# Average pooling over a row: loads and stores issued from GpSimd in place of SyncE

## The chip, the cores and the metric

The kernel runs on one core of a Trainium2 chip. The metric is the device time of one execution in microseconds (us), as the median of several runs. A profiled execution gives the trace; its "span" is the time from the first to the last recorded instruction. In the profile the engines are called PE (TensorE), DVE (VectorE), ACT (ScalarE), POOL (GpSimd) and SP (SyncE). A name with a q at the end, such as SPq or POOLq, is the sequencer of that engine, which handles instructions that are not computation: waits, barriers and the issue of DMA transfers.

## The reference

The input x is 32 x 256 x 4096 in float32, 134.2 MB. Each row of 4096 is cut into 256 windows of 16 neighbours, and the output holds the mean of every window, 32 x 256 x 256, 8.4 MB.

```python
def reference(x, output_size):                     # output_size = 256
    ...
    for i in range(output_size):
        start = int(i * length / output_size)
        end = int((i + 1) * length / output_size)
        result[:, :, i] = np.mean(x[:, :, start:end], axis=-1)
```

## The kernel before

The 32 x 256 = 8192 rows are worked off in 16 tiles of 512 rows. A tile has 128 partitions with 4 rows (65,536 bytes) each, so one load moves 8.39 MB. In SBUF a tile is seen as 128 partitions x 1024 windows ("cells") x 16 elements. The pool `inpool` has two buffers of that size, and the loads go to them in turn: load t + 2 needs the buffer of load t.

The loop `for t in range(ntiles)` does the following for each tile:

- line 70 issues the load into `xin`, on SP;
- line 73, on POOL, folds the second half of the windows (cells 512 to 1023): the upper 8 elements of each window are added onto the lower 8;
- line 78, on DVE, sums the 16 elements of each window in the first half;
- line 81, on DVE, sums the 8 remaining elements of each window in the second half, and so waits for line 73;
- line 84, on ACT, multiplies the tile's 1024 sums by 1/16.

The first fifteen tiles write their results into one large buffer, `res_many`, which a single store of 7,680 KB takes out. This store stands in the last turn of the loop, in the text between the load of the last tile and the computation on it. The last tile writes into `res_last`, and two stores, of 120 and of 8 partitions, take that out after the loop. All three stores go through the helper `store` (line 58). It issues the DMA, excludes it from the semaphores that the tile framework manages (`no_tile_sem_insts`) and lets it raise a semaphore of its own, `stored`, by 16.

The tile framework records the instructions while the kernel's text runs. When the context is compiled (`tc.compile()`), it fixes the order of each engine's queue and puts in the waits. Each engine then works its queue off in that order. In the kernel before, SP's queue holds only the issues of the loads and stores, and POOL's queue only the adds of line 73, apart from constants at the start and the closing barrier, which the profile shows under line 94. After that barrier SP waits until `stored` has reached 48, that is, until all three stores have landed, and clears it.

Of the kernel before, what the change touches and what calls it, by code (L numbers as in the profile page):

```python
# [1 line left out]

# [4 lines left out]


@with_exitstack
def kernel(  # L10
    ctx: ExitStack,
    tc: tile.TileContext,
    x: bass.AP,
    output_size: int,
    out: bass.AP,
):

    nc = tc.nc
    F32 = mybir.dt.float32
    X = mybir.AxisListType.X

    batch, channels, length = x.shape
    ob, oc, olen = out.shape
    assert ob == batch and oc == channels and olen == output_size
    assert length % output_size == 0
    window = length // output_size  # L30
    hw = window // 2
    inv_w = 1.0 / float(window)

    P = nc.NUM_PARTITIONS
    R = 4
    rows = batch * channels
    assert rows % (P * R) == 0
    ntiles = rows // (P * R)
    many = (ntiles - 1) * R
    cells = R * output_size  # L40
    m = cells // 2
    cols = R * length

    xr = x.rearrange("b c l -> (b c) l")
    orow = out.rearrange("b c o -> (b c) o")
    x_many = xr[0 : P * many, :].rearrange("(p r) l -> p (r l)", p=P, r=many)
    o_many = orow[0 : P * many, :].rearrange("(p r) o -> p (r o)", p=P, r=many)
    x_last = xr[P * many :, :].rearrange("(p r) l -> p (r l)", p=P, r=R)
    o_last = orow[P * many :, :].rearrange("(p r) o -> p (r o)", p=P, r=R)

    res_many = nc.alloc_sbuf_tensor("res_many", [P, (ntiles - 1) * cells], F32, align_bytes=256)
    res_last = nc.alloc_sbuf_tensor("res_last", [P, cells], F32, align_bytes=256)
    inpool = ctx.enter_context(tc.tile_pool(name="inpool", bufs=2))

    stored = nc.alloc_semaphore("stored")

    def store(out, in_):
        ins = nc.sync.dma_start(out=out, in_=in_)
        tc.no_tile_sem_insts.add(ins.ins.name)
        ins.then_inc(stored, 16)  # L60

    for t in range(ntiles):
        last = t == ntiles - 1
        xin = inpool.tile([P, cells, window], F32, name="xin")
        if last:
            res, base, src = res_last, 0, x_last
        else:
            res, base = res_many, t * cells
            src = x_many[:, t * cols : (t + 1) * cols]
        nc.sync.dma_start(out=xin.rearrange("p o w -> p (o w)"), in_=src)  # L70
        if last:
            store(o_many, res_many[:, :])
        nc.gpsimd.tensor_add(  # L73
            out=xin[:, m:cells, 0:hw],
            in0=xin[:, m:cells, 0:hw],
            in1=xin[:, m:cells, hw:window],
        )
        nc.vector.reduce_sum(  # L78
            out=res[:, base : base + m], in_=xin[:, 0:m, :], axis=X
        )  # L80
        nc.vector.reduce_sum(  # L81
            out=res[:, base + m : base + cells], in_=xin[:, m:cells, 0:hw], axis=X
        )
        nc.scalar.mul(  # L84
            out=res[:, base : base + cells],
            in_=res[:, base : base + cells],
            mul=inv_w,
        )
    for lo, hi in ((0, 120), (120, P)):
        store(o_last[lo:hi, :], res_last[lo:hi, :])  # L90

    ctx.pop_all().close()
    tc.close()
    tc.compile()  # L94
    nc.sync.wait_ge(stored, 48)
    nc.sync.sem_clear(stored)


# [1 line left out]
_INS = ['x', 'output_size']  # L100
_OUTS = [((32, 256, 256), 'float32')]

_NUMBERS = {'output_size': 256}


# [26 lines left out]
```

## Time and profile before

| what | value |
|---|---|
| median of 3 runs | 333.5 us (333.32 to 333.67) |
| the profiled execution | 333.37 us, its span 332.1 us |
| DVE busy | 209.7 us, 63% of the span |
| POOL busy | 139.7 us, 42% |
| ACT busy | 18.2 us, 5% |
| HBM read and written | 134.22 MB and 8.39 MB, 429 GB/s over the span |

Busy time counts computing instructions only; waits, barriers and the issue of a DMA do not count. "DMA share" is the mean busy share of the core's 16 DMA engines. In lists of waits, a line names the instruction that waited, what released it, the total time, how often, and the longest. A row for an instruction group gives the shape of output and input, the count, the busy time and the mean of one. A load's "time to landing" runs from its issue to the signal that its data has arrived. These are the groups of computing instructions in the loop:

```profile
L73 POOL TENSOR_TENSOR xin<-xin 128x4096 f32<-128x4096 f32 x16 | 139.5, 8719 | 181.7 <-DMA xin<-in_x_dram 181.7
L78 DVE TENSOR_REDUCE res_many<-xin 128x512 f32<-128x8192 f32 x15 | 130.3, 8686 | 107.4 <-DMA xin<-in_x_dram 107.4
L81 DVE TENSOR_REDUCE res_many<-xin 128x512 f32<-128x4096 f32 x15 | 66.3, 4420 | 2.5 <-POOL xin L73 2.3
L84 ACT ACTIVATE res_many<-res_many 128x1024 f32<-128x1024 f32 x15 | 15.9, 1057 | 289.8 <-DVE res_many L81 289.8
```

### The profile page before, as it was taken

What the parts mean: (1) busy time and instruction counts of PE and PEld (TensorE: products, weight loads), DVE (VectorE), ACT (ScalarE), POOL (GpSimd) and SP (SyncE); (2) the same over time, 40 slices, a digit from 0 to 9 for tenths busy, and PEclk for the clock granted to TensorE, in tenths of its full rate; (3) what the DMA queues carried; (4) which work ended last, traced back from release to release, by engine and by line L of the source; (5) the groups of instructions that cost most, each with busy time, mean ns of one, the idle gap of its engine ahead of it and who ended that gap; (6) DMA issues with size and microseconds to landing.
All of it is one profiled execution on the core that took longest, in us unless ns stands there. A gap on an engine that the chain in (4) does not pass through costs nothing.

```text
span 332.1 us, 160 instructions
## 1 busy us (share of the span) xinstructions
DVE 209.7 (63%) x32; ACT 18.2 (5%) x17; POOL 139.7 (42%) x20
## 2 busy tenths in 40 slices
DVE  0029396692939669293966939295693929569392
ACT  1000101001010100101010010101000010100001
POOL 0027091542709164270916427090643709063270
DMA  9898999989899998989899998989999898989997
GB/s 379 379 505 379 474 411 426 458 379 505 379 489 395 450 434 379 505 379 505 379 474 411 395 489 379 505 379 489 395 450 434 379 505 379 505 379 474 395 466 307
DMA packets 2599, 142.61 MB, mean 429 GB/s; under 512 B 295, under 2 KB 295, under 8 KB 423
## 3 DMA queue, kind: packets, MB, share of 16 engines
q1 hardware_dynamic: 2599, 142.61, 99.4%
HBM read 134.22 MB, written 8.39 MB: 429 GB/s over the span
## 4 chain that ended last, share of the span: by engine, by line
DMA 66%; POOL 18%; DVE 11%; POOLq 3%; issue 0%; ACT 0%; SPq 0%
DMA xin<-in_x_dram 66%; POOL xin L73 18%; DVE res_many L81 9%; POOLq L94 3%; DVE res_last L81 1%; ACT res_last L84 0%; SPq L70 0%; POOLq L73 0%
## 5 line engine op out<-in xcount | busy, mean ns | idle before, releaser
L73 POOL TENSOR_TENSOR xin<-xin 128x4096 f32<-128x4096 f32 x16 | 139.5, 8719 | 181.7 <-DMA xin<-in_x_dram 181.7
L78 DVE TENSOR_REDUCE res_many<-xin 128x512 f32<-128x8192 f32 x15 | 130.3, 8686 | 107.4 <-DMA xin<-in_x_dram 107.4
L81 DVE TENSOR_REDUCE res_many<-xin 128x512 f32<-128x4096 f32 x15 | 66.3, 4420 | 2.5 <-POOL xin L73 2.3
L84 ACT ACTIVATE res_many<-res_many 128x1024 f32<-128x1024 f32 x15 | 15.9, 1057 | 289.8 <-DVE res_many L81 289.8
L78 DVE TENSOR_REDUCE res_last<-xin 128x512 f32<-128x8192 f32 x1 | 8.7, 8686 | 6.3 <-DMA xin<-in_x_dram 6.3
L81 DVE TENSOR_REDUCE res_last<-xin 128x512 f32<-128x4096 f32 x1 | 4.4, 4420 | 0.2 <-POOL xin L73 0.2
L84 ACT ACTIVATE res_last<-res_last 128x1024 f32<-128x1024 f32 x1 | 1.1, 1057 | 18.5 <-DVE res_last L81 18.5
L84 ACT ACT_TABLE_LOAD x1 | 1.3, 1283 | 0.7 <-PEq L113 0.7
L113 POOL MEMSET const-float32-0.0<- 128x1 f32 x1 | 0.1, 99 | 0.2 <-issue 0.2
L113 POOL MEMSET const-bfloat16-1.0<- 128x1 bf16 x1 | 0.1, 103 | 0.0
L113 POOL MEMSET const-uint8-127<- 128x1 uint8 x1 | 0.1, 103 | 0.0
L113 POOL MEMSET const-float32-1.0<- 128x1 f32 x1 | 0.1, 99 | 0.0
## 6 DMA issues: line engine op xcount, KB each, us to landing
out_dram<-res_many SPq DMA_DIRECT2D x1, 7680.0 KB
out_dram<-res_last SPq DMA_DIRECT2D x1, 480.0 KB
xin<-in_x_dram SPq DMA_DIRECT2D x16, 25.3
out_dram<-res_last SPq DMA_DIRECT2D x1, 32.0 KB
```

The source lines that it names most:

```text
L73: nc.gpsimd.tensor_add(out=xin[:, m:cells, 0:hw], in0=xin[:, m:cells, 0:hw], in1=xin[:, m:cells, hw:window],)
L78: nc.vector.reduce_sum(out=res[:, base : base + m], in_=xin[:, 0:m, :], axis=X)
L81: nc.vector.reduce_sum(out=res[:, base + m : base + cells], in_=xin[:, m:cells, 0:hw], axis=X)
L84: nc.scalar.mul(out=res[:, base : base + cells], in_=res[:, base : base + cells], mul=inv_w,)
L94: tc.compile()
L113: nc = _bacc.Bacc("TRN2", target_bir_lowering=False, num_devices=1)
```

## The change

The two places that issue a DMA, the helper `store` and the load in the loop, name GpSimd in place of SyncE. What is moved, the shapes, the two buffers and the computation stay as they are. SP keeps the wait for `stored` and its clearing at the end.

```diff
     def store(out, in_):
-        ins = nc.sync.dma_start(out=out, in_=in_)
+        ins = nc.gpsimd.dma_start(out=out, in_=in_)
         tc.no_tile_sem_insts.add(ins.ins.name)
         ins.then_inc(stored, 16)
...
-        nc.sync.dma_start(out=xin.rearrange("p o w -> p (o w)"), in_=src)
+        nc.gpsimd.dma_start(out=xin.rearrange("p o w -> p (o w)"), in_=src)
```

## The prediction

> **What bounds the kernel now.** I read the table of queues first, then stretches of the timeline with their DMA share, then the waits of SP's own queue beside the chain of waits, and last the instructions at both ends. The queue and the stretches:
>
> ```profile
> q1 hardware_dynamic: 2599, 142.61, 99.4%
> 22.70:42.00 19.30, 13.11 (x2) 1.06 (x1) 8.72 (x1) 1.00 1.00 435
> 42.00:312.90 270.90, 183.52 (x29) 14.80 (x14) 122.07 (x14) 1.00 1.00 433
> 327.30:332.10 4.80, 0.00 (x0) 0.00 (x0) 0.00 (x0) 1.00 0.74 314
> ```
>
> The columns of the last three rows are the length of the stretch, the busy time of DVE, ACT and POOL with counts, PE's clock, the DMA share and GB/s. In the loop the 16 DMA engines are always busy, at 433 to 435 GB/s. The add of load 1 starts at 42.05 us and that of load 15 at 312.97, so one load takes 270.92 / 14 = 19.35 us. DVE has 13.1 us of work per load and POOL 8.7; neither sets that pace. What SP waits for, one period of the chain in order of time, and the loads themselves:
>
> ```profile
> SPq L70 <- DVE res_many L81: 185.8, 14, 13.3
> ...
> 80.72 0.02 issue
> 80.74 0.02 POOLq L73
> 80.76 0.09 issue
> 80.85 8.73 POOL xin L73
> 89.58 0.02 issue
> 89.60 4.43 DVE res_many L81
> 94.03 0.02 issue
> 94.05 25.30 DMA xin<-in_x_dram
> ...
> L70 SPq DMA_DIRECT2D xin<-in_x_dram x16: 327/328/413, 0.7 to 287.3; - x16
> DMA to landing us min/median/max: 22.0/25.3/40.8
> ```
>
> The load of this period has landed at 80.72, and its buffer is released 94.05 - 80.72 = 13.3 us later. The next load is then in flight for another 19.35 - 13.3 = 6.0 us. So each issue comes 6.0 us before the engines would run dry, and 25.3 us to landing is 6.0 of queueing plus 19.35 of transfer. The shortest time to landing, 22.0 us with nothing ahead, leaves 22.0 - 19.35 = 2.7 us for issue, first bytes and the semaphore. These 2.7 us are covered by the 6.0 in the loop; 3.3 us of cover remain.
>
> **The change part by part.** The sum is made against the profiled execution: span 332.1, time 333.37, so 1.3 us lie around the span; 333.37 is 0.13 below the median of 333.5.
>
> First, removed: nineteen issues on SP (sixteen loads at 0.33 to 0.41 us, one store at 0.35, two at 0.74 together). SP computes nothing and nobody waits for it but the DMA, so this gives back only what stands at the ends. The same nineteen issues are added to POOL's queue, which already holds sixteen adds.
>
> Second, the price of one issue on POOL, which no row shows. From below: POOL's shortest instruction, MEMSET, 0.10 us, so a gain of 0.3 at the first load. From above: POOL's longest, the add, 8.72 us, a loss of 8.4. The nearest row is the same operation on SP, 0.41 at the first load; since it is not the same engine I raise the fixed 2.7 us by a quarter: 0.7 us more than on SP, about 1.1 per issue. At the first load nothing covers it, because all engines idle until the first landing: +0.7.
>
> Third, the fourteen later loads. Their wait for DVE's release moves to POOL's queue. If load t+2 stands there between add t and add t+1, POOL waits at it from the end of add t (landing + 8.75) to the release (landing + 13.3), issues in about 1.1 us, and has 19.35 - 13.3 - 1.1 = 4.9 us left before add t+1 can start. Queued behind the wait is only that add, and DVE's second reduction waits for it; neither is late. The added 0.7 lies under the 3.3 us of cover: 0. With the cover gone each microsecond counts fourteen times. At the upper bound an issue is 8.4 longer, 5.1 beyond the cover, or 14 x 5.1 = 71 us.
>
> Fourth, the big store. In the timeline its data is ready at 307.67, load 15 lands at 312.86 and add 15 cannot begin earlier: 5.2 us of cover against 1.1. Cost 0.
>
> Fifth, the end. These rows are the last issues, the drains of the closing barrier and SP's last wait:
>
> ```profile
> 327.26 0.74 SPq L58 DMA_DIRECT2D out_dram<-res_last  x2
> ...
> L94 SPq EVENT_SEMAPHORE  x6: 17/28/28, 328.1 to 329.0; - x6
> L94 POOLq DRAIN  x3: 34/83/8811, 312.9 to 328.8; - x3
> L94 SPq DRAIN  x3: 7/7/7, 328.3 to 328.6; - x3
> ...
> SPq L96 <- DMA out_dram<-res_last: 3.0, 1, 3.0
> ```
>
> The big store, 7,680 KB, occupies the engines for 7.86 MB / 434 GB/s = 18.1 us from 312.86, so to about 331.0. The two small stores, issued at 327.26, only have to stand in the queue by then: 3.7 us of cover against twice 1.1, cost 0. The barrier is different. Now it runs from 328.1 to 329.0 while the stores are still moving, and SP's wait of 3.0 us comes after it. POOL's drain in this barrier is a new risk. From below: SP's drain takes 7 ns with SP's own stores in flight, so a drain need not wait for DMAs: 0. From above: POOL's drain held 8,811 ns, until POOL's last add was over; if it likewise holds until the DMAs that POOL issued are through, the whole barrier moves behind the last landing: 329.0 - 328.1 = +0.9. I take the upper value, because that row is of the same engine. What is late next is only SP's clear of the semaphore.
>
> Sum: 0.7 + 0 + 0 + 0 + 0.9 = 1.6; 333.37 + 1.6 = 335.0, and on the median 333.5 + 1.6 = 335.1.
>
> A rule speaks against the change. The adds take 8,717 to 8,722 ns in all sixteen cases, each beside a DVE reduction of 8.69 us, and DVE is idle for 6.0 us when a later load is issued. The Trainium skill (SBUF — State Buffer, section "SBUF: two separate sides") says that a DMA issued from GpSimd is starved of descriptors while VectorE holds the shared port in a 2-port mode. No row here shows such blocking; were it to hold for these reductions, the moment of issue would still miss them, and the sum would stay. The same skill (DMA: Bandwidth & Descriptors, "Latency and other measured facts") puts the first byte at about 1 us from GpSimd and 600 ns from SP; by it the first term would be 0.4 and the time 334.8, an estimate from that page.
>
> **The rivals.** The decisive unknown is the order in POOL's queue, which the build fixes and the page of before cannot show, since there the loads stand alone on SP. My forecast takes it that the framework queues an instruction when what it needs is there, so that load 1 comes before add 0 and load t+2 before add t+1.
>
> Rival one, pairs: two loads, then two adds. Load 2, free at landing 0 + 13.3, then stands behind add 1, which begins only at the next landing. For: nothing in the page forbids it. Against: add 1 has to wait 6.0 us longer than load 2. It decides as soon as a load stands behind an add that waits for a later landing. Price: the engines run dry and start again 8.73 (add) + 22.0 (alone to landing) + 0.7 after the landing, that is 31.4 in place of 19.35, +12.1 once per pair, so 7 x 12.1 = 85 us: 420; if the big store stands behind add 15 as well, 8.7 + 2.7 + 0.7 = 12 more: 432. I put it at 426.
>
> Rival two, the order of the text: load, add, load, add. It is how the loop is written. Every later load pays 12.1: 15 x 12.1 = 181, so 335 + 181 = 516.
>
> Rival three, software pace: the order is good, but an issue or the packets that it makes are dearer. The whole 8.72 at the first load gives 333.5 + 8.4 + 0.9 = 343; packets 2% slower cost 16 x 19.35 x 0.02 = 6, so 341. Against: the page shows 435 GB/s with packets of 65 KB (142.61 MB in 2,599), so little is decided per packet.
>
> Rival four, on the other side: not slower. Place: the two ends. POOL's issue costs no more than SP's 0.41 us and its drain no more than SP's 7 ns; the price is 0 and the time 333.5. It decides when both terms together stay under 0.67 us. For: SP's drain row. Against: POOL's. That the change doesn't do what it says is no case here: the two edited calls are the only issues there are.
>
> **How the numbers follow.** Chances: forecast 0.61, own range 334.0 to 336.8 (from a third of the sum to about twice the sum above 333.5); rival one 0.11, rival two 0.08, rival three 0.09, rival four 0.11. The time is the forecast's, 335.1. The range reaches down to rival four with the scatter of the runs, 333.1, and up through rival three with both its prices a little exceeded, 346; outside are rivals one and two, 0.19. A measurement of this kernel can tell about 0.2%, 0.67 us, from no change. Slower is above 334.17: 0.59 of the forecast's 0.61, and rivals one to three, 0.28; together 0.87. Same, 332.83 to 334.17: 0.02 of the forecast and 0.08 of rival four, 0.10. Faster: the rest of rival four, 0.03, where POOL's issue comes at its lower bound.
>
> **What would show it.** The order is seen at once: the second load issued within some 2 us of the first, the adds 19.35 us apart, the DMA share at 1.00 in the loop. A first landing at about 23.4 in place of 22.7 shows the first term. A barrier after the last landing, POOL's long drain ending there and SP's wait near 0 show the last. Adds alternately 31 and 19 us apart mean rival one, all 31 apart rival two, an even pace above 19.4 rival three. The forecast is wrong above all if a load stands behind an add.

## The result, and the profile after

The changed kernel takes 465.93 us as a median (465.88 to 466.14) against 333.51 before: a ratio of 1.397, 95% interval 1.395 to 1.400. The forecast was 335.1, its range 333.1 to 346.

The page of the changed kernel, engines and queue:

```profile
DVE 208.2 (45%) x32; ACT 18.2 (4%) x17; POOL 150.2 (32%) x39
q0 software_dynamic: 2624, 142.61, 72.2%
```

The same 142.61 MB now keep the DMA engines busy for 72.2% of the span, where it was 99.4%. The profile lists POOL's queue as `software_dynamic` and the one that SP used before as `hardware_dynamic`. The busy time of DVE and ACT is as before, and POOL has only gained the issues, 39 instructions in place of 20: on POOL the profile does count an issue as busy time, 10.5 of the 150.2 us, unlike on SP. So no computation has grown; time has been added in which nothing moves. One period of the loop in stretches (length, busy time of DVE, ACT, POOL with counts, PE's clock, DMA share, GB/s):

```profile
42.80:56.10 13.30, 13.30 (x3) 0.25 (x1) 8.72 (x1) 1.00 0.00 0
56.10:78.20 22.10, 4.07 (x2) 1.86 (x2) 1.10 (x2) 1.00 1.02 427
78.20:97.50 19.30, 8.67 (x2) 0.00 (x0) 8.71 (x1) 1.00 0.88 380
```

For 13.3 us after the landing at 42.80 the DMA share is 0.00. A load with nothing ahead of it then takes 22.1 us from issue to landing, and a second one lands 19.3 us later. Two loads take 54.8 us ((426.34 - 42.80) / 7, from landing 1 to landing 15) in place of 38.7. The timeline shows what the first of them waited for:

```profile
42.80 8.69 DVE L78 TENSOR_REDUCE res_many<-xin 128x512 f32<-128x8192 f32 x1 [10.60 <-DMA xin<-in_x_dram]
42.85 8.72 POOL L73 TENSOR_TENSOR xin<-xin 128x4096 f32<-128x4096 f32 x1 [10.57 <-DMA xin<-in_x_dram]
51.40 8.74 DVE L81 TENSOR_REDUCE res_many<-xin 128x512 f32<-128x4096 f32 x2
55.85 1.06 ACT L84 ACTIVATE res_many<-res_many 128x1024 f32<-128x1024 f32 x1 [53.82 <-DVE res_many L81]
56.11 0.58 POOL L70 DMA_DIRECT2D xin<-in_x_dram  x1 [4.54 <-DVE res_many L81]
...
60.44 0.53 POOL L70 DMA_DIRECT2D xin<-in_x_dram  x1 [3.76 <-DVE res_many L81]
...
78.17 8.69 DVE L78 TENSOR_REDUCE res_many<-xin 128x512 f32<-128x8192 f32 x1 [18.03 <-DMA xin<-in_x_dram]
```

Tile 0 landed at 23.51 and was added by 32.3, yet its second sum (line 81) does not run until 51.4, together with that of tile 1 ("x2"). DVE's queue holds the first sum of tile 1 ahead of it, and that one waits for landing 1. Only at 55.8 is the buffer of tile 0 free. On POOL, load 2 stands behind add 1, which also waits for landing 1. This is POOL's queue as listed from the built programs (+ added, - removed; ISA is the instruction that the trace calls MODIFY_POOL_CONFIG):

```
+L70 DMACopy xin<-in_x_dram 128x16384 x2
 L73 ISA
-L73 TensorTensor xin<-xin 128x512x8 x16
+L73 TensorTensor xin<-xin 128x512x8 x2
+L70 DMACopy xin<-in_x_dram 128x16384 x2
+L73 TensorTensor xin<-xin 128x512x8 x2
...
+L58 DMACopy out_dram<-res_many 128x15360
+L58 DMACopy out_dram<-res_last 120x1024
+L58 DMACopy out_dram<-res_last 8x1024
```

DVE's queue has changed too, though the diff doesn't name it: the first sums of two tiles now stand together, then their second sums, as the timeline above shows; before, they stood tile by tile.

The end, in the list of the barrier's line:

```profile
L94 SPq DRAIN  x3: 7/7/7, 444.8 to 463.9; - x3
L94 POOLq DRAIN  x3: 34/96/18159, 445.5 to 464.1; - x3
```

Of POOL's three drains one holds for 18.2 us, from 445.5 to 463.7, while the stores move. The barrier comes after it.

The 132.3 us that the span has grown by are then: 0.8 at the first landing (23.51 against 22.72), 7 x 16.1 = 112.7 in the loop, and 18.8 from the last landing to the end (38.1 against 19.2). Around the span there are 1.7 us in place of 1.3.

### The profile page after: what moved, and what is told of

Read it like the earlier page. It is cut to its first block, busy times and chain, and to the rows that moved or that the text cites. A ratio compares the mean times of both kernels' runs of the same rounds, so it can differ in the third digit from the quotient of the medians.

```text
span 464.4 us, 132 instructions
## 1 busy us (share of the span) xinstructions
DVE 208.2 (45%) x32; ACT 18.2 (4%) x17; POOL 150.2 (32%) x39
## 2 busy tenths in 40 slices
DMA packets 2624, 142.61 MB, mean 307 GB/s; under 512 B 320, under 2 KB 320, under 8 KB 448
## 3 DMA queue, kind: packets, MB, share of 16 engines
q0 software_dynamic: 2624, 142.61, 72.2%
## 4 chain that ended last, share of the span: by engine, by line
DMA 65%; DVE 29%; DVEq 1%; issue 1%; POOL 0%; ACT 0%; POOLq 0%; PEldq 0%
DMA xin<-in_x_dram 65%; DVE res_many L81 14%; DVE res_many L78 13%; DVE res_last L78 2%; DVEq L94 1%; ACT res_last L84 0%; POOL xin L70 0%; POOL out_dram L58 0%; POOLq L94 0%; PEldq L94 0%
## 5 line engine op out<-in xcount | busy, mean ns | idle before, releaser
L70 POOL DMA_DIRECT2D xin<-in_x_dram x16 | 8.9, 558 | 59.0 <-DVE res_many L81 58.1
L58 POOL DMA_DIRECT2D out_dram<-res_last x2 | 1.0, 524 | 3.8 <-ACT res_last L84 3.8
```

Of the source, the lines that this page charges most:

```text
L58: ins = nc.gpsimd.dma_start(out=out, in_=in_)
L70: nc.gpsimd.dma_start(out=xin.rearrange("p o w -> p (o w)"), in_=src)
```

## Experiments

Two theories. Order: the places of the loads, adds and sums in the two queues cost nearly everything, and issuing from POOL costs little. Source: transfers that come from POOL are themselves late or slow.

**POOL as the source, with the order held.** The loop's text is rearranged so that load t + 2 is traced after tile t, and each instruction on POOL and DVE is pinned behind the one traced before it on its engine.

```diff
...                                 # load, add, sum_a, sum_b and scale as functions
+    xins = [load(0), load(1)]
     for t in range(ntiles):
+        add(xins[t])                  # each POOL and DVE instruction:
+        sum_a(t, xins[t])             # tc.keep_in_program_order(...)
+        sum_b(t, xins[t])
+        scale(t)
+        if t + 2 < ntiles:
+            xins.append(load(t + 2))  # nc.gpsimd.dma_start
+        if t == ntiles - 2:
+            store(o_many, res_many[:, :])
```

> All loads and stores on POOL as in the changed kernel, but POOL's order is held to load t+2 ahead of add t+1 and DVE's to first sum, second sum, tile by tile. Theory (order): the 132 us come from the order in the two queues and the issue on POOL itself costs little, so about 335.2 us: 333.5, +0.8 for the later first landing, +0.9 if the closing barrier waits for the stores; landings 19.35 us apart. Rival (source): transfers issued from POOL are themselves late or slow whatever the order, so still above 440 us.

Measured: 336.56 us, ratio 1.009 (1.008 to 1.011). The source theory falls. The loop in its stretch, and the end in the list of the barrier's line:

```profile
42.00:313.90 271.90, 183.49 (x29) 14.79 (x14) 129.87 (x28) 1.00 1.01 435
```

```profile
L116 POOLq DRAIN  x3: 39/96/5225, 328.9 to 334.6; - x3
L116 POOLq EVENT_SEMAPHORE  x4: 17/17/17, 334.2 to 334.8; - x4
```

All sixteen loads come from POOL and the engines run at 435 GB/s without a gap; landings 0 and 15 are at 23.67 and 313.90, 19.35 us apart each, the pace of the kernel before. The order theory holds, but its sum was 1.4 us short, which the last experiments split up.

**The order without POOL as the source.** Loads and stores stay on SP; DVE is pinned to two first sums, then two second sums. POOL's adds are pinned as well, but only in the order of the tiles.

```diff
-    for t in range(ntiles):
+    for t0 in range(0, ntiles, 2):
+        xins = [load(t0), load(t0 + 1)]          # nc.sync.dma_start
+        for k in (0, 1): add(xins[k])            # pinned
+        for k in (0, 1): sum_a(t0 + k, xins[k])  # pinned
+        for k in (0, 1): sum_b(t0 + k, xins[k])  # pinned
+                         scale(t0 + k)
...                                              # the big store behind scale 14
```

> Nothing issued from POOL: loads and stores on SP as before the change, but DVE's order is that of the changed kernel, the first sums of two tiles and then their second sums. Order: the release of the first buffer of a pair comes 13.1 us after the second landing, the engines run dry, 54.5 us per pair, some 464 us in all. Source: 333.5 us, as nothing comes from POOL.

Measured: 458.61 us, ratio 1.375 (1.373 to 1.377), 5 us under the expected 464. One period in stretches:

```profile
42.04:55.08 13.04, 13.04 (x3) 0.00 (x0) 8.72 (x1) 1.00 0.00 0
55.08:76.87 21.79, 4.30 (x2) 2.11 (x2) 0.00 (x0) 1.00 1.03 433
76.87:96.19 19.32, 8.69 (x2) 0.00 (x0) 8.72 (x1) 1.00 0.88 380
```

The same picture as in the changed kernel, with no transfer from POOL at all. So DVE's order by itself accounts for 458.61 - 333.53 = 125.1 of the 132.4 us. The other 7.3 are what is left for issuing from POOL: 0.55 per pair ((421.70 - 42.04) / 7 = 54.24 us from landing 1 to landing 15, against 54.79), 7 x 0.55 = 3.9 that shows because nothing covers it any more, 0.7 at the first landing and the rest behind the last.

**One queue put right at a time.** Two kernels with everything on POOL. In the first only DVE's sums are pinned, tile by tile (the diff below shows the first of the two sums); the second is the held order of the first experiment without the pins on DVE, so that only POOL's queue has load t + 2 ahead of add t + 1. DVE's queue is then neither tile by tile nor in pairs: the build puts each second sum behind the first sum of the next tile.

```diff
-        nc.vector.reduce_sum(
+        tc.keep_in_program_order(nc.vector.reduce_sum(
             out=res[:, base : base + m], in_=xin[:, 0:m, :], axis=X
-        )
+        ))
...
```

> All DMAs on POOL, DVE held to first sum, second sum, tile by tile; POOL's queue keeps two loads, two adds. If POOL's order alone sets the release: the third load goes out when add 1 is over, 8.75 us after the second landing, and lands 22.1 later, 50.2 us per pair; with the big store behind the last add some 426 us. If DVE's order adds nothing to it: 466 us, as in the changed kernel.

> All DMAs on POOL, POOL held to load t+2 ahead of add t+1; DVE's queue is left to the build, which puts the first sum of tile t+1 ahead of the second sum of tile t. Order: the release of every buffer now waits for the next landing, 13.2 us after it, and the add of that next tile stands behind the load, 35.5 us per load, some 575 us. If POOL's order is what matters: 335 us.

Measured, one time each: 427.78 and 578.34 us. In the first, load 2 goes out the moment add 1 is over, as the timeline shows:

```profile
32.44 4.42 DVE L81 TENSOR_REDUCE res_many<-xin 128x512 f32<-128x4096 f32 x1
...
42.95 8.72 POOL L73 TENSOR_TENSOR xin<-xin 128x4096 f32<-128x4096 f32 x1 [10.54 <-DMA xin<-in_x_dram]
51.61 0.57 POOL L70 DMA_DIRECT2D xin<-in_x_dram  x1
51.70 4.42 DVE L81 TENSOR_REDUCE res_many<-xin 128x512 f32<-128x4096 f32 x1
```

Its buffer had been free since 36.9 (32.44 + 4.42). In the second, the timeline shows the two queues working against each other:

```profile
42.77 8.69 DVE L82 TENSOR_REDUCE res_many<-xin 128x512 f32<-128x8192 f32 x1 [10.61 <-DMA xin<-in_x_dram]
51.37 4.41 DVE L88 TENSOR_REDUCE res_many<-xin 128x512 f32<-128x4096 f32 x1
55.81 1.06 ACT L94 ACTIVATE res_many<-res_many 128x1024 f32<-128x1024 f32 x1 [53.79 <-DVE res_many L88]
56.08 0.58 POOL L67 DMA_DIRECT2D xin<-in_x_dram  x1 [23.84 <-DVE res_many L88]
56.67 8.73 POOL L71 TENSOR_TENSOR xin<-xin 128x4096 f32<-128x4096 f32 x1
78.09 8.69 DVE L82 TENSOR_REDUCE res_many<-xin 128x512 f32<-128x8192 f32 x1 [22.31 <-DMA xin<-in_x_dram]
```

Load 2 stands in the right place on POOL and waits there 23.84 us, because the second sum of tile 0 stands on DVE behind the first sum of tile 1. The add of tile 1, landed at 42.77, now stands behind that load and begins at 56.67. Every load is issued after the landing before it, and a landing comes every 35.4 us ((538.54 - 42.77) / 14). With POOL's queue put right and DVE's left to the build, the kernel is slower than with both in pairs. The two orders don't add up: pairs on POOL alone cost 91 us over the held order (427.78 against 336.56), pairs on DVE alone 125, and both together 129 (465.93 against 336.56), because a load goes out when the later of the two lets it.

**The order of the text.** POOL's loads, adds and stores pinned to the order of the text: load, add, load, add.

```diff
-        nc.gpsimd.dma_start(out=xin.rearrange("p o w -> p (o w)"), in_=src)
+        tc.keep_in_program_order(nc.gpsimd.dma_start(out=..., in_=src))
...
-        nc.gpsimd.tensor_add(
+        tc.keep_in_program_order(nc.gpsimd.tensor_add(
...
```

> All DMAs on POOL, held to the order of the text, load t and then add t. Order: every load goes out 8.75 us after the landing before it and lands 22.1 later, 30.9 us per load, 15 times 11.5 more than in the loop before, some 508 us. Source: near the changed kernel's 466 us.

Measured, one time: 510.48 us. Landings 0, 1 and 2 are at 23.55, 54.38 and 85.17, 30.8 us apart.

**The same issues on another queue that computes.** Both edited calls name ACT (`nc.scalar.dma_start`), nothing is pinned.

> The same nineteen issues moved to ACT's queue, which also computes (the scale of each tile), with nothing held by hand; the build puts load t+2 right behind scale t. Order: load t+2 goes out when scale t is over, 14.4 us after the landing in place of 13.3, 1.1 later under a cover of 3.3, so 333.5 to 334.2 us. Source (any queue that also computes is slow): well above 340 us.

Measured: 333.68 us, ratio 1.0006 (0.9997 to 1.0014): no change that can be told. The timeline:

```profile
36.09 1.06 ACT L84 ACTIVATE res_many<-res_many 128x1024 f32<-128x1024 f32 x1 [33.16 <-DVE res_many L81]
36.16 0.33 ACTq L70 DMA_DIRECT2D xin<-in_x_dram  x1
42.14 8.69 DVE L78 TENSOR_REDUCE res_many<-xin 128x512 f32<-128x8192 f32 x1 [6.09 <-DMA xin<-in_x_dram]
```

The build put load 2 right behind scale 0, and ACT's queue issues it at 36.16 while the scale is still running, so not even the expected 1.1 us were lost. DVE's queue stayed tile by tile. So it isn't enough that a computing engine issues; what differs is the order that the build chose. ACT's transfers, unlike POOL's, are listed as `hardware_dynamic`, but the held order shows that POOL's kind is no slower in the loop.

**Another tiling on POOL.** The changed kernel with `R = 2` (2 rows per partition) and four buffers in place of two, nothing pinned.

> The changed kernel with tiles of half the size (2 rows per partition, 32 tiles) and four buffers, nothing held by hand. The build's order on POOL is then two loads, two adds, two loads, and from there on add t ahead of load t+2, with one more load always in flight; DVE's sums stand tile by tile after the first pair. Order: one dry stretch at the first pair (4.4 of add + 12.4 alone to landing - 9.7 = 7.1) and one at the end, where the big store stands behind the last add (about 6): 336.6 + 13 = 350 us. Source: at least the changed kernel's 466 us, since twice as many loads come from POOL.

Measured: 352.03 us, ratio 1.056 (1.054 to 1.057). The two dry stretches are where they were expected, from the timeline:

```profile
23.67 4.45 POOL L73 TENSOR_TENSOR xin<-xin 128x2048 f32<-128x2048 f32 x1 [5.19 <-DMA xin<-in_x_dram]
27.96 4.47 DVE L81 TENSOR_REDUCE res_many<-xin 128x256 f32<-128x2048 f32 x2
28.07 1.10 POOL L70 DMA_DIRECT2D xin<-in_x_dram  x2
40.66 4.42 DVE L78 TENSOR_REDUCE res_many<-xin 128x256 f32<-128x4096 f32 x1 [8.23 <-DMA xin<-in_x_dram]
...
321.91 4.45 POOL L73 TENSOR_TENSOR xin<-xin 128x2048 f32<-128x2048 f32 x1 [5.21 <-DMA xin<-in_x_dram]
326.30 0.58 POOL L58 DMA_DIRECT2D out_dram<-res_many  x1
```

And between them, in stretches:

```profile
42.00:324.00 282.00, 195.27 (x59) 18.27 (x29) 144.29 (x58) 1.00 0.99 428
```

Twice as many loads from POOL cost 114 us less than in the changed kernel, because from the third tile on there is always one more load in flight. So the order that the build chooses is not fixed by the engine alone. Tile size and number of buffers changed together here; which of the two made the difference was not tried. The order was enough to price the kernel within about 2 us.

**The rest: start and end.** Three kernels in which everything is in the order of before: the held order with the stores on SP; the held order with the loads on SP and the stores on POOL; and the kernel before with only the two small stores on POOL.

```diff
-    def store(out, in_):
-        ins = nc.sync.dma_start(out=out, in_=in_)
+    def store(out, in_, eng, sem):     # third kernel
+        ins = eng.dma_start(out=out, in_=in_)
...
+            store(o_many, res_many[:, :], nc.sync, stored)
...
+        store(o_last[lo:hi, :], res_last[lo:hi, :], nc.gpsimd, stored_b)
```

> As the run with the held order, with the three stores back on SP. Order: only the late first landing is left, 334.3 us, and the closing barrier again runs while the stores move. Source: the loads come from POOL, so still above 440 us.

> As the run with the held order, with the sixteen loads back on SP and the three stores on POOL. If POOL's drain in the closing barrier waits for the stores that POOL issued: 334.4 us, with a long drain that ends after the last landing. If it does not: 333.5 us.

> The kernel before with only the two small stores of the last tile issued from POOL, on a semaphore of their own; loads and the big store stay on one queue of SP. If the 3 us of the run with all stores on POOL came from the end (drain and barrier after the last landing, and the longer time outside the span): load 15 lands at 312.9 us as before and the time is 335.4, +1.5 in the span and +0.45 around it. If they came from load 15 sharing the engines with a big store of another queue: 333.5 us.

Measured: 335.30 (ratio 1.0055, 1.0041 to 1.0069), 336.53 (1.0091, 1.0077 to 1.0104) and 335.34 us (1.0056, 1.0042 to 1.0070). The first two missed by 1.0 and 2.1 us, and together they add up to 4.8 where the kernel that has both moves costs 3.0. The third points to why. Its timeline and the second kernel's at the last landing:

```profile
307.59 0.35 SPq L59 DMA_DIRECT2D out_dram<-res_many  x1
312.87 8.69 DVE L79 TENSOR_REDUCE res_last<-xin 128x512 f32<-128x8192 f32 x1 [6.39 <-DMA xin<-in_x_dram]
```

```profile
307.90 0.74 POOL L58 DMA_DIRECT2D out_dram<-res_many  x1 [5.85 <-ACT res_many L94]
315.16 8.69 DVE L82 TENSOR_REDUCE res_last<-xin 128x512 f32<-128x8192 f32 x1 [8.65 <-DMA xin<-in_x_dram]
```

With load 15 and the big store on one queue the load lands at 312.87; with the store on another queue, 2.3 us later. With the parts exchanged (loads on POOL, store on SP) it is 316.38 against 313.90, 2.5 later. The computation on the last tile then ends later, and its small stores are issued later, at 329.83 in the second kernel against 327.55 in the third. The Trainium skill (DMA: Bandwidth & Descriptors, "Queues, rings and completion order") says that each DMA engine goes round between the queues that have work; these landings agree with that. Two things limit the reading. The two queues were always SP's and POOL's, so of different kinds; two queues of one kind were not tried. And one queue is no full protection: in the order of the text, where the store is issued 5.9 us after load 15 on the same queue, that load took 23.4 us to landing; the median there is 22.2. That the later landing makes up the whole of the two misses was not tried by itself.

The third kernel has no such mixture at its last load, and its 1.85 us (335.34 against 333.49) belong to the end alone. In the list of the barrier's line:

```profile
L95 POOLq DRAIN  x3: 34/88/5000, 328.0 to 333.4; - x3
L95 POOLq EVENT_SEMAPHORE  x4: 17/17/17, 333.0 to 333.6; - x4
```

POOL's drain ends at 333.0, where the barrier was over at 329.0 before. In the first kernel, whose loads come from POOL and whose stores come from SP, POOL's drain was over at 326.5, although the stores moved on until about 334: it holds for the DMAs that POOL issued. In the profiled execution the third kernel's span grows by 1.7 us (333.8 against 332.1); by the medians of all runs it grows by 1.5 (333.7 against 332.2), and the other 0.35 us lie around the span. There, every kernel whose last stores come from POOL takes 1.67 to 1.75 us in the profiled execution; in the others it is 1.26 to 1.45.

## Why the prediction was wrong, point by point

- **What bounds the kernel:** right. 19.35 us per load, 13.3 to the release and 5.8 to 6.0 of lead returned in the held order and on ACT.
- **The step that failed** is the assumption that "the framework queues an instruction when what it needs is there, so that load 1 comes before add 0 and load t+2 before add t+1". Load 1 did come before add 0, but load 2 was put behind add 1. It got 0.61, and the pairs 0.11. With the order that it assumed held by hand, on POOL and on DVE, the time is 336.56 us; the build's order in the two queues makes it 465.93. The cover that the third part counted on, 3.3 us for each load, was gone for every second load.
- **Rival one had the right order on POOL and missed DVE.** It gave 426; with DVE held tile by tile the run took 427.78. That the two agree so well is partly luck: 426 lies midway between 420 and 432, and since the big store did stand behind add 15, the sum to compare is 432. It is 4 too high, because a pair was priced at 31.4 + 19.35 = 50.75 us and took 50.1. The part left unpriced is an engine that the diff does not name: its queue was rearranged too, and the next load goes out 13.3 us after the second landing in place of 8.7. A pair takes 54.8 us against 50.1 with DVE held, 7 x 4.7 = 33 us more in the loop. At the end the big store goes out 14.4 us after the last landing in place of 8.7, which makes 5.6 us. Together that is the way from 428 to 466.
- **Rival two:** 516 forecast, 510.48 measured with that order. The price of an issue in the open was some 0.5 too high per load: 31.4 us forecast, 30.9 measured. With nothing ahead, a load from POOL lands after 21.9 us at the shortest in this kernel, where the sum has 22.0 + 0.7.
- **Rival three:** its 343 leaves out the 71 us that the third part works out for an issue as long as an add. Its 65 KB per packet holds only without the 423 packets under 8 KB; 142.61 MB in 2,599 packets is 55 KB. Nothing rests on either, since an issue stayed far under that length.
- **The price of an issue on POOL:** 1.1 us taken, 0.53 to 0.71 measured. The first landing came 0.8 to 1.0 later, forecast 0.7; the issue begins at 1.27 in place of 0.74. The rest lies between issue and landing, 22.24 us for the first load from POOL and 21.98 from SP; in the other kernels with loads of this size from POOL it is 22.2 to 22.4. The Trainium skill (DMA: Bandwidth & Descriptors, "Latency and other measured facts") has 0.4 us between the two at the first byte; the 0.2 to 0.4 here are of that size.
- **The loop's cover:** right. In the held order the longer way costs nothing (19.35). With the cover gone it cost 0.55 per pair.
- **The end:** the mechanism was right, POOL's drain holds until the stores are through. The size was 0.9 and is 1.85. The barrier behind the drain is what was priced, 0.8 us (333.0 to the end of the span at 333.8) against 0.9. Not in the sum were the 0.35 around the span and the small stores' later landing: they were put at nothing, but from POOL they are issued 0.3 us later (327.55 against 327.26) and need 4.6 to 4.9 us to landing; the barrier waits for that now.
- **The port rule** of the Trainium skill (SBUF — State Buffer, "SBUF: two separate sides") did not bite, but not for the reason argued. The prediction had every later issue miss the sums on DVE; in the changed kernel the first load of each pair is issued beside a running sum (56.11). Its issue took 0.58 us like the others, it landed 22.06 us later, and no sum on DVE became longer (8.69 and 4.41 to 4.42 us). Whether these sums use a 2-port mode no row shows.
- **Why the build chose pairs** is open. The runs show that the order differs with the issuing engine (ACT) and with the tiling (tile size and buffers together); what it goes by was not tried.

## What to carry to other kernels

Before moving DMA issues onto an engine that computes, list all the queues of the built program, those of untouched engines too: a load that stands behind an instruction waiting for a later landing loses its lead, and the price can be worked out from the order and the durations of the changed kernel's trace (426, 350, 508, 575 and 464 us were forecast so, and 427.78, 352.03, 510.48, 578.34 and 458.61 measured, so within 2 to 5 us). If the issues have to be there, hold the order by hand on every engine that takes part in the release of the buffer; one alone can be worse than none (578.34 us, measured one time). What the move costs apart from the order was 3.0 us here, all at the two ends.

## What was not expected of the hardware

- A load that shares the DMA engines with a big store landed 2.3 to 2.5 us earlier when both stood in one queue than when they stood in two, SP's and POOL's.
- DMAs issued by POOL moved as fast as SP's: 435 GB/s in the loop. With nothing ahead and the same order on DVE, a load took 22.0 us at the shortest from issue to landing from POOL and 21.8 from SP.
- A drain on POOL held for DMAs that POOL had issued (3.6 to 19.6 us in the kernels whose last stores came from POOL), while SP's drain took 7 ns with SP's own stores in flight.
- ACT's queue issued a load 0.07 us after the scale before it had begun, so a running ACTIVATE did not hold back the issue behind it.
